# Strassen-Winograd MLP: the last group's combinations moved from GpSimd to VectorE and spread over the products, row and column factor in one instruction

## The chip, the cores and the metric

The kernel runs on one core of a Trainium2 chip. The metric is the device time of one execution in microseconds. Each kernel is timed in several runs; the kernel before has a median of 1384.01 us over 3 runs (1383.27 to 1384.59). A profiled execution gives the trace, with instruction starts counted from the start of its span.

## The reference

A decoder layer on x (1024 tokens x 1024 features, all float32): a mixer (state-space heads and stick-breaking attention heads), cross-attention to 256 memory tokens, a squared-ReLU MLP, each added to the residual h, and one final RMSNorm. The change lies in the MLP's second product and the final norm:

```python
def rmsnorm(x, g):
    y = xf * lax.rsqrt(jnp.mean(xf * xf, axis=-1, keepdims=True) + EPS)
    return (y * g)

def sqrelu_mlp(hn, w1, w2):
    u = hn @ w1                       # 1024 x 4096
    u = jnp.square(jax.nn.relu(u))
    return u @ w2                     # 1024 x 1024

h = h + sqrelu_mlp(rmsnorm(h, norm_ff_g), w_ff1, w_ff2)
return rmsnorm(h, final_g)
```

## The kernel before

The MLP uses the Strassen-Winograd scheme for 2 x 2 blocks: seven block products in place of eight, with sums and differences of blocks before and after them. Each float32 operand is split into a high part (`whi`, a rounded copy made by ScalarE) and a low part (`wlo`, the difference, made by VectorE, line 109), and a product of two operands is three matmuls (lines 207 to 209): high by high, high by low, low by high.

The first stage, a loop over 16 pairs `p` of feature blocks (from line 1165), computes u and stores, for each pair, seven combinations of its blocks in DRAM (`ud`: A11, A12, A22, S1, S2, S3, S4). The four combinations S1, S3, S2, S4 are made on GpSimd (`SE`, line 1163).

The second stage (line 1284) runs over two groups `g` of 8 pairs. In each group come seven products (`prod2`) in the order S3, S1, S2, A11, A22, S4, A12. A product has 8 pairs of operands (one loaded from `ud`, the other a combination of w2's blocks, made in place on VectorE), four row tiles `tb` of 128 rows, and three matmuls for each pair and row tile: 96 matmuls of 128x512. Its four results lie in four PSUM banks; two sets of four banks alternate. When a product is done, `accumulate` adds each bank to its targets: S3's to A7, S1's to A5, S2's to U2, A11's to U2 and C11, A22's is taken off C21, S4's is added to C12 and A12's to C11. C11, C12 and C21 start from the residual h, which three DMAs of 1 MB bring in (line 1226, ahead of both groups).

In the last group (`fin`), after the fourth product, the combinations follow: A7 += U2, C21 += A7 on GpSimd, A7 += A5 and A7 += c22 on VectorE, where c22 is the residual of the fourth quarter, loaded there (line 1322); A7 then holds C22. After the fifth product the final norm of rows 4 to 7 (the lower half: C21 and C22) is worked out, and A5 += U2 and C12 += A5 run on GpSimd. After the seventh product, `last` adds each row tile of C11 and finishes rows 0 to 3. Its matmuls are ordered so that each row tile's last three pairs run together (`NLAST`), so the four row tiles end one after another.

The final norm of a row tile: ScalarE's `squares` sums the squares of each half into the two columns of a small tile `st`; `rows_out` (line 1269) adds them, scales, takes the power -0.5 on GpSimd, and multiplies each half by the row factor `st[:, 3:4]` before the store on SP's queue. The multiplication by the column factor (`gained`, the gain `gfin`) goes ahead of it, on GpSimd or VectorE.

The order of instructions on each engine is worked out when the program is built: a planner takes, among the instructions that are ready in its own model of the time, the one that comes first in the program. `later(by)` moves a stretch in this order: `later(-EARLY)` (3000 places earlier) puts loads and splits of operands ahead, `later(-TB * tb)` does so for the last row tiles. On the chip each engine then works through its list strictly in order. The splits run ahead of the matmuls as far as six buffers of `whi` and `wlo` allow, three pairs of operands.

Of the kernel before, what the change touches and what calls it, by code (L numbers as in the profile page):

```python
# [13 lines left out]
ALU = mybir.AluOpType  # L14
AX = mybir.AxisListType

P = 128
# [22 lines left out]
XQ2 = 1  # L40
XSC = 0
# [49 lines left out]
def hybrid_trunk(ctx: ExitStack, tc: tile.TileContext, xT, x, cols, rows, gain, fing, wzd, wp, out):  # L91
# [1071 lines left out]
    SE = nc.gpsimd  # L1163
    h1 = hp.tile([P, 2, 4, 512], F32, tag="h1", name="w1r2")
    for p in range(NPR):
# [39 lines left out]
        store_u(p, "A22", a22_)  # L1205
        add(s1, a21_, a22_, SE)
# [18 lines left out]
    for c, r, n in ((accs[0][:, 0], 0, 0), (accs[0][:, 1], 0, 1), (accs[1][:, 0], 1, 0)):  # L1225
        nc.sync.dma_start(out=c, in_=hd[rows[r], rows[n]].rearrange("(a p) n -> p a n", p=P))
# [20 lines left out]
    def into(*targets, first=False, sign=ALU.add):  # L1247
        def accumulate(tb, ps):
            for c in targets:
                if first:  # L1250
                    act(c[tb], ps)
                else:
                    tt(c[tb], c[tb], ps, sign)
        return accumulate
# [8 lines left out]
    def gained(t, c, n, eng, gfin):  # L1263

        o = dt_("c", NCB)
        tt(o, c[t % 4], gfin[:, 512 * n:512 * n + 512], ALU.mult, eng)
        return o

    def rows_out(t, obs, st):
        tt(st[:, 2:3], st[:, 0:1], st[:, 1:2], ALU.add)  # L1270
        ts(st[:, 2:3], st[:, 2:3], 1.0 / D, EPS, ALU.mult, ALU.add)
        nc.gpsimd.tensor_tensor(out=st[:, 3:4], in0=st[:, 2:3], in1=nhalf[:, 0:1], op=ALU.pow)
        for n, ob in enumerate(obs):
            ts(ob, ob, st[:, 3:4], None, ALU.mult)
            nc.sync.dma_start(out=out[t * P:(t + 1) * P, 512 * n:512 * n + 512], in_=ob)
# [8 lines left out]
    for g in range(NG):  # L1284
# [25 lines left out]
        if fin:  # L1310
            pl_, tag = slots[2]
            gfin = pl_.tile([P, 2, 4, 512], F32, tag=tag, name="gfin")[:, 0, 0:2].rearrange("p a n -> p (a n)")
            nc.scalar.dma_start(out=gfin, in_=fing.partition_broadcast(P))
        prod2(q, both("S3", lambda a, b, c, d: sub(dt_(("u2", "u3")[next_(nd)], 2), d, b), load),
              into(A7, first=first))
        prod2(q + 1, both("S1", lambda a, b, c, d: sub(b, b, a)), into(A5, first=first))
        prod2(q + 2, both("S2", lambda a, b, c, d: sub(b, d, b)), into(U2, first=first))
        prod2(q + 3, both("A11", lambda a, b, c, d: a), into(U2, C11))
        if fin:
            c22 = [dt_("c", NCB) for _ in range(4)]  # L1320
            for tb in range(4):
                nc.sync.dma_start(out=c22[tb], in_=hd[512 + tb * P:512 + (tb + 1) * P, 512:1024])
                add(A7[tb], A7[tb], U2[tb], nc.gpsimd)
                add(C21[tb], C21[tb], A7[tb], nc.gpsimd)
                tt(A7[tb], A7[tb], A5[tb], ALU.add)
                tt(A7[tb], A7[tb], c22[tb], ALU.add)
        prod2(q + 4, both("A22", lambda a, b, c, d: sub(b, b, c)), into(C21, sign=ALU.subtract))
        if fin:
            for tb in range(4):
                t = 4 + tb  # L1330
                st = squares(t, C21, 0, squares(t, A7, 1))
                rows_out(t, (gained(t, C21, 0, nc.vector, gfin), gained(t, A7, 1, nc.gpsimd, gfin)), st)
                add(A5[tb], A5[tb], U2[tb], nc.gpsimd)
                add(C12[tb], C12[tb], A5[tb], nc.gpsimd)
        prod2(q + 5, both("S4", lambda a, b, c, d: d), into(C12))

        if fin:
            sts = [squares(tb, C12, 1) for tb in range(4)]
            g12 = [gained(tb, C12, 1, nc.gpsimd, gfin) for tb in range(4)]

        def last(tb, ps):
            with later(-TB * tb):
                tt(C11[tb], C11[tb], ps, ALU.add)
                if fin:
                    squares(tb, C11, 0, sts[tb])
                    rows_out(tb, (gained(tb, C11, 0, nc.vector if tb >= GV else nc.gpsimd, gfin), g12[tb]), sts[tb])
# [66 lines left out]
```

## Time and profile before

| | |
|---|---|
| median of 3 runs | 1384.01 us |
| the profiled execution's own time | 1381.92 us |
| its span | 1380.2 us |
| TensorE (PE) busy | 1313.0 us, 95% |
| VectorE (DVE) busy | 972.9 us, 70% |
| ScalarE (ACT) busy | 685.3 us, 50% |
| GpSimd (POOL) busy | 235.6 us, 17% |
| TensorE's granted clock, mean | 0.991 of full speed |

Busy shares are averages over stages with different limits. The stages that the change touches are the end of the first stage (about 1020 to 1080), and the last group of the second stage with the final norm (about 1200 to 1380). PE is TensorE's matmuls and PEld its weight loads; SP only issues DMAs. A matmul of 128x512 shows a duration of about 0.39 us, but they are pipelined and start about 0.23 us apart.

### The profile page before, as it was taken

How to read it: one execution, taken by the hardware profiler on the slowest of the kernel's cores; microseconds unless marked ns; L12 is line 12 of the kernel's file. 1: busy time of each engine (PE TensorE's matmuls, PEld its weight loads, DVE VectorE, ACT ScalarE, POOL GpSimd, SP SyncE). 2: the span in 40 equal slices, each digit the busy share in tenths (PEclk: the TensorE clock that was granted, in tenths of full speed). 3: DMA queues.
4: the chain of work that ended last, by engine and by line, in shares of the span. 5: the costliest groups of instructions: out<-in, count | busy, mean ns of one | idle time of the engine just before them, and what ended most of it. 6: DMA issues, size and time to landing. Idle time of an engine off the chain costs nothing.

```text
span 1380.2 us, 18343 instructions
## 1 busy us (share of the span) xinstructions
PE 1313.0 (95%) x6469; PEld 1065.1 (77%) x6469; DVE 972.9 (70%) x1521; ACT 685.3 (50%) x1304; POOL 235.6 (17%) x238
## 2 busy tenths in 40 slices
PE   9999999899998999999898999999999999999987
PEld 7989977687776778887676888888887888888765
DVE  7748864676789765628789666666659855677896
ACT  7355642565567542626555545554444544444343
POOL 0000002210211010000263323321331000000543
PEclk9999999999999999999998999999999999999999
DMA  6111355842656433111224445444368933633232
GB/s 216 39 62 48 103 152 132 240 117 66 168 162 203 132 108 104 47 31 31 92 77 146 167 153 168 131 144 153 130 208 297 320 113 92 236 92 94 75 124 90
DMA packets 95852, 181.68 MB, mean 132 GB/s; under 512 B 9808, under 2 KB 14992, under 8 KB 95760
## 3 DMA queue, kind: packets, MB, share of 16 engines
q1 hardware_dynamic: 85184, 156.04, 35.3%
q0 software_dynamic: 8624, 18.88, 4.9%
q10 hardware_dynamic: 1952, 5.58, 1.1%
q8 instruction: 51, 0.84, 0.2%
q14 instruction: 41, 0.34, 0.1%
HBM read 128.00 MB, written 52.46 MB: 131 GB/s over the span
## 4 chain that ended last, share of the span: by engine, by line
PE 72%; DVE 12%; issue 6%; ACT 4%; DMA 3%; POOL 2%; POOLq 0%; SPq 0%; DVEq 0%; ACTq 0%
PE P L207 7%; PE P L209 7%; PE P L208 7%; PE pr L207 6%; PE pr L208 6%; PE pr L209 6%; DVE stay L738 3%; DVE wlo L109 3%; PE o L209 2%; PE o L207 2%; PE o L208 2%; DMA wst<-in_wp 2%; PE ops L769 1%; PE wT L755 1%; PE qkps L207 1%
## 5 line engine op out<-in xcount | busy, mean ns | idle before, releaser
L208 PE MATMUL pr<-wlo,whi 128*128 128x512 f32 x448 | 177.7, 397 | 11.4 <-DVE wlo L109 11.3
L207 PE MATMUL pr<-whi 128*128 128x512 f32 x448 | 176.4, 396 | 0.7 <-ACT whi L106 0.7
L209 PE MATMUL pr<-whi,wlo 128*128 128x512 f32 x448 | 177.0, 395 | 0.0
L109 POOL TENSOR_TENSOR c<-c 128x512 f32<-128x512 f32 x64 | 88.9, 1400 | 247.6 <-ACT c L106 223.8
L208 PEld LDWEIGHTS pr<-wlo,whi 128*128 128x128 f32 x448 | 84.3, 188 | 35.2 <-DVE wlo L109 15.9
L109 DVE TENSOR_TENSOR wlo<-w1r,whi 128x512 fp32r<-128x512 f32 x92 | 80.7, 878 | 39.9 <-ACT whi L106 39.7
L106 ACT ACTIVATE whi<-w1r 128x512 fp32r<-128x512 f32 x92 | 58.0, 631 | 94.6 <-PE P L208 62.6
L207 PE MATMUL P<-T,whi 128*128 128x512 f32 x256 | 101.6, 397 | 2.0 <-ACT T L106 2.0
L209 PE MATMUL P<-T,wlo 128*128 128x512 f32 x256 | 101.2, 395 | 0.0
L208 PE MATMUL P<-T,whi 128*128 128x512 f32 x256 | 101.0, 394 | 0.0
L207 PEld LDWEIGHTS pr<-whi 128*128 128x128 f32 x448 | 84.3, 188 | 21.1 <-ACT whi L106 1.1
L209 PEld LDWEIGHTS pr<-whi,wlo 128*128 128x128 f32 x448 | 84.3, 188 | 19.7
L106 ACT ACTIVATE c<-c 128x512 f32<-128x512 f32 x128 | 78.7, 628 | 26.4 <-DVE c L109 25.0
L738 DVE TENSOR_TENSOR_SCAN stay<-stay,dg 128x128 f32<-128x128 f32 (+3 forms) x64 | 84.8, 1346 | 3.9 <-ACT stay L106 3.8
L106 ACT ACTIVATE whi<-wst 128x512 fp32r<-128x512 f32 (+1 forms) x88 | 54.1, 628 | 65.3 <-PE o L209 24.6
L106 ACT ACTIVATE whi<-us 128x512 fp32r<-128x512 f32 x64 | 40.3, 629 | 82.9 <-PE pr L208 74.2
L207 PE MATMUL P<-B,whi 128*128 128x512 f32 x192 | 76.8, 400 | 0.0
L208 PE MATMUL P<-B,whi 128*128 128x512 f32 x192 | 76.4, 398 | 0.0
L209 PE MATMUL P<-B,wlo 128*128 128x512 f32 x192 | 76.3, 397 | 0.0
L109 DVE TENSOR_TENSOR wlo<-wst,whi 128x512 fp32r<-128x512 f32 (+1 forms) x88 | 60.5, 705 | 20.8 <-ACT whi L106 20.5
L109 DVE TENSOR_TENSOR wlo<-pair,whi 128x512 fp32r<-128x512 f32 x96 | 74.4, 775 | 0.0
L109 DVE TENSOR_TENSOR wlo<-us,whi 128x512 fp32r<-128x512 f32 x64 | 47.6, 744 | 36.1 <-ACT whi L106 35.9
(332 smaller groups left out, 3425.6 us busy)
## 6 DMA issues: line engine op xcount, KB each, us to landing
ud<-c SPq DMA_DIRECT2D x112, 256.0 KB, 2.5
wst<-in_wp SPq DMA_DIRECT2D x104, 256.0 KB, 2.8
w1r<-in_wp SPq DMA_DIRECT2D x16, 1024.0 KB, 6.4
us<-ud SPq DMA_DIRECT2D x64, 256.0 KB, 2.6
pair<-in_wp SPq DMA_DIRECT2D x16, 1024.0 KB, 6.5
kk<-kd POOLq DMA_DIRECT2D x32, 256.0 KB, 5.1
p<-ud SPq DMA_DIRECT2D x24, 256.0 KB, 2.6
u<-ud SPq DMA_DIRECT2D x24, 256.0 KB, 2.6
```

Of the source, the lines that this page charges most:

```text
L106: nc.scalar.activation(out=out, in_=in_, func=func, **kw)
L109: (eng or nc.vector).tensor_tensor(out=out, in0=a, in1=b, op=op)
L207: nc.tensor.matmul(out=ps, lhsT=a[0], rhs=b[0], start=start, stop=False)
L208: nc.tensor.matmul(out=ps, lhsT=a[0], rhs=b[1], start=False, stop=False)
L209: nc.tensor.matmul(out=ps, lhsT=a[1], rhs=b[0], start=False, stop=stop)
L738: nc.vector.tensor_tensor_scan(out=stay[:, 0:W][:, ::-1], data0=stay[:, 0:W][:, ::-1], data1=B.dg1[:, S - W:S][:, ::-1], initial=0.0, op0= ...
L755: nc.tensor.transpose(out=t4[:, o:o + P], in_=wb[ii][:, b * P:(b + 1) * P], identity=ident)
L769: nc.tensor.matmul(out=ops[:, oc:oc + 256], lhsT=v, rhs=w[:, sb * 256:sb * 256 + 256], start=(s2_ == 0 and sb == 0 and j == 0), stop=(last ...
```

## The change

The last group's combinations all run on VectorE, each behind the product that gives its summand: after S3, C21 and C22 get A7; after S1, C12 and C22 get A5; after A11, C22, C21 and C12 get U2. C22 is now a tile of its own, loaded with the residual before the last group's first product. `then` calls these additions for each row tile, `AFT` = 24 places later in the order. The first stage's last pair makes its four combinations on VectorE. The loads of C11, C12 and C21 are issued behind the first group's second product. In the final norm, `rows_out` multiplies by row and column factor in one VectorE instruction (`stt`, line 115) in place; for the last row tile alone the column factor goes ahead, VectorE scales one half and ScalarE the other, which is stored by ScalarE's queue. `squares` and `rows_out` of rows 4 to 7 are also `AFT` places later.

```diff
+AFT = 24
-    SE = nc.gpsimd
...
+        SE = nc.gpsimd if p < NPR - 1 else nc.vector
         add(s1, a21_, a22_, SE)
...
-    for c, r, n in ((accs[0][:, 0], 0, 0), (accs[0][:, 1], 0, 1), (accs[1][:, 0], 1, 0)):
-        nc.sync.dma_start(out=c, in_=hd[rows[r], rows[n]].rearrange("(a p) n -> p a n", p=P))
...
-    def into(*targets, first=False, sign=ALU.add):
+    def into(*targets, first=False, sign=ALU.add, then=None):
...
+            if then is not None:
+                with later(AFT):
+                    then(tb)
...
+    def rows_out(t, cs, st):
+
+        factor(t, st)
+        for n, c in enumerate(cs):
+            stt(c[t % 4], c[t % 4], st[:, 3:4], gfin[:, 512 * n:512 * n + 512], ALU.mult, ALU.mult)
+            store_rows(t, n, c[t % 4])
...
+        C22 = [dt_("c", NCB) for _ in range(4)] if fin else None
+
+        def plus(c, a):
+            def go(tb):
+                for c_ in c:
+                    add(c_[tb], c_[tb], a[tb])
+            return go if fin else None
+
+        if fin:
+            for tb in range(4):
+                nc.sync.dma_start(out=C22[tb], in_=hd[512 + tb * P:512 + (tb + 1) * P, 512:1024])
         prod2(q, both("S3", lambda a, b, c, d: sub(dt_(("u2", "u3")[next_(nd)], 2), d, b), load),
-              into(A7, first=first))
-        prod2(q + 1, both("S1", lambda a, b, c, d: sub(b, b, a)), into(A5, first=first))
+              into(A7, first=first, then=plus((C21, C22), A7)))
+        prod2(q + 1, both("S1", lambda a, b, c, d: sub(b, b, a)),
+              into(A5, first=first, then=plus((C12, C22), A5)))
+        if first:
+            for c, r, n in ((accs[0][:, 0], 0, 0), (accs[0][:, 1], 0, 1), (accs[1][:, 0], 1, 0)):
+                nc.sync.dma_start(out=c, in_=hd[rows[r], rows[n]].rearrange("(a p) n -> p a n", p=P))
         prod2(q + 2, both("S2", lambda a, b, c, d: sub(b, d, b)), into(U2, first=first))
-        prod2(q + 3, both("A11", lambda a, b, c, d: a), into(U2, C11))
-        if fin:
-            c22 = [dt_("c", NCB) for _ in range(4)]
-            for tb in range(4):
-                nc.sync.dma_start(out=c22[tb], in_=hd[512 + tb * P:512 + (tb + 1) * P, 512:1024])
-                add(A7[tb], A7[tb], U2[tb], nc.gpsimd)
-                add(C21[tb], C21[tb], A7[tb], nc.gpsimd)
-                tt(A7[tb], A7[tb], A5[tb], ALU.add)
-                tt(A7[tb], A7[tb], c22[tb], ALU.add)
+        prod2(q + 3, both("A11", lambda a, b, c, d: a), into(U2, C11, then=plus((C22, C21, C12), U2)))
...
-            for tb in range(4):
-                t = 4 + tb
-                st = squares(t, C21, 0, squares(t, A7, 1))
-                rows_out(t, (gained(t, C21, 0, nc.vector, gfin), gained(t, A7, 1, nc.gpsimd, gfin)), st)
-                add(A5[tb], A5[tb], U2[tb], nc.gpsimd)
-                add(C12[tb], C12[tb], A5[tb], nc.gpsimd)
+            with later(AFT):
+                for tb in range(4):
+                    st = squares(4 + tb, C21, 0, squares(4 + tb, C22, 1))
+                    rows_out(4 + tb, (C21, C22), st)
...
-                    squares(tb, C11, 0, sts[tb])
-                    rows_out(tb, (gained(tb, C11, 0, nc.vector if tb >= GV else nc.gpsimd, gfin), g12[tb]), sts[tb])
+                    st = squares(tb, C11, 0, sts[tb])
+                    if tb < 3:
+                        rows_out(tb, (C11, C12), st)
+                    else:
+                        g11 = gained(C11[tb], 0)
+                        factor(tb, st)
+                        ts(g11, g11, st[:, 3:4], None, ALU.mult)
+                        act(g12, g12, scale=st[:, 3:4])
+                        store_rows(tb, 0, g11)
+                        nc.scalar.dma_start(out=out[tb * P:(tb + 1) * P, 512:1024], in_=g12)
```

## Rows read from the trace of the kernel before

**Rows 1.** The page's chain that ended last, shares of the span by engine.

```profile
PE 72%; DVE 12%; issue 6%; ACT 4%; DMA 3%; POOL 2%; POOLq 0%; SPq 0%; DVEq 0%; ACTq 0%
```

**Rows 2.** Stretches: us, each engine's busy us (instructions), PEclk, DMA share, GB/s.

```profile
1060.00:1100.00 40.00, 39.33 (x169) 31.41 (x169) 34.59 (x54) 23.16 (x42) 1.54 (x1) 1.00 0.92 313
1222.90:1245.20 22.30, 22.30 (x97) 18.02 (x96) 17.93 (x29) 9.23 (x16) 0.00 (x0) 1.00 0.32 95
1245.20:1267.50 22.30, 22.30 (x97) 18.02 (x96) 17.20 (x28) 9.23 (x16) 0.00 (x0) 1.00 0.32 96
1267.50:1289.80 22.30, 22.30 (x97) 18.02 (x96) 12.66 (x21) 9.22 (x16) 0.00 (x0) 1.00 0.32 95
1289.80:1326.00 36.20, 27.74 (x111) 20.99 (x110) 36.20 (x33) 11.79 (x24) 31.32 (x19) 0.95 0.20 58
```

**Rows 3.** Waits of PE and PEld, 1289 to 1372: us, times, longest.

```profile
PE pr L208 <- DVE wlo L109: 9.2, 6, 3.2
...
PEld pr L208 <- DVE wlo L109: 13.0, 8, 3.6
```

**Rows 4.** Order of time, last group: start us, us, instruction [idle before].

```profile
1267.54 1.88 DVE L109 TENSOR_TENSOR acc<-acc,pr 128x512 f32<-128x512 f32 x3
...
1289.83 1.88 DVE L109 TENSOR_TENSOR acc<-acc,pr 128x512 f32<-128x512 f32 x3
...
1299.35 1.78 DVE L109 TENSOR_TENSOR wlo<-pair,whi 128x512 fp32r<-128x512 f32 x1
...
1300.55 1.75 POOL L109 TENSOR_TENSOR c<-c,acc 128x512 f32<-128x512 f32 x1
...
1301.06 0.68 DVE L109 TENSOR_TENSOR acc<-acc,pr 128x512 f32<-128x512 f32 x1
```

**Rows 5.** Order of time: the last product's end and after it.

```profile
1369.87 0.40 PE L209 MATMUL pr<-whi,wlo 128*128 128x512 f32 x1
...
1367.24 1.98 DVE L113 TENSOR_SCALAR c<-c,fst 128x512 f32<-128x512 f32 x2
...
1370.54 0.68 DVE L109 TENSOR_TENSOR acc<-acc,pr 128x512 f32<-128x512 f32 x1
...
1374.92 0.14 DVE L113 TENSOR_SCALAR fst<-fst 128x1 f32<-128x1 f32 x1
...
1375.15 0.55 POOL L1272 TENSOR_TENSOR fst<-fst,nhalf 128x1 f32<-128x1 f32 x1 [1.13 <-DVE fst L113]
...
1375.73 0.88 DVE L113 TENSOR_SCALAR c<-c,fst 128x512 f32<-128x512 f32 x2 [0.66 <-POOL fst L1272]
```

**Rows 6.** Order of time: between the first and second stage.

```profile
1052.14 2.39 DVE L109 TENSOR_TENSOR u<-pair 128x512 f32<-128x512 f32 x2
1054.45 1.78 DVE L109 TENSOR_TENSOR pair<-pair 128x512 f32<-128x512 f32 x1
1056.16 1.75 DVE L109 TENSOR_TENSOR wlo<-us,whi 128x512 fp32r<-128x512 f32 x1
...
1052.52 4.84 POOL L109 TENSOR_TENSOR c<-c 128x512 f32<-128x512 f32 x3 [22.86 <-ACT c L106]
...
1058.57 0.50 PE L208 MATMUL pr<-wlo,whi 128*128 128x512 f32 x1 [2.13 <-DVE wlo L109]
```

**Rows 7.** Order of time: first load of C11, C12, C21.

```profile
1087.85 0.37 SPq L1226 DMA_DIRECT2D acc<-hd  x1
```

**Rows 8.** Groups by line and form: names, count | busy us, mean ns.

```profile
L116 DVE SCALAR_TENSOR_TENSOR h<-o,ry,h 128x512 f32<-128x512 f32 x16 | 12.0, 747 | 7.6 <-PE o L209 7.4
...
L109 POOL TENSOR_TENSOR c<-acc,gfin 128x512 f32<-128x512 f32 x6 | 8.6, 1446 | 18.6 <-DVE acc L109 18.6
...
L109 POOL TENSOR_TENSOR c<-c,gfin 128x512 f32<-128x512 f32 x4 | 6.4, 1620 | 0.0
...
L106 ACT ACTIVATE u<-acc 128x512 f32<-128x512 f32 x4 | 2.5, 631 | 8.1 <-DVE acc L109 7.2 <-DVE fst L113 0.9
L106 ACT ACTIVATION_READ_ACCUMULATOR u<-acc 128x1 f32 x4 | 0.7, 186 | 0.0
```

More of the change, by code (lines that the diff above doesn't have):

```diff
@@ L1261, in squares, with factor @@
         return st
[L1263 to L1269, printed above, removed]
+    def factor(t, st):
         tt(st[:, 2:3], st[:, 0:1], st[:, 1:2], ALU.add)
@@ L1272, in rows_out, with store_rows, gained @@
         nc.gpsimd.tensor_tensor(out=st[:, 3:4], in0=st[:, 2:3], in1=nhalf[:, 0:1], op=ALU.pow)
-        for n, ob in enumerate(obs):
-            ts(ob, ob, st[:, 3:4], None, ALU.mult)
-            nc.sync.dma_start(out=out[t * P:(t + 1) * P, 512 * n:512 * n + 512], in_=ob)
+    def store_rows(t, n, c):
+        nc.sync.dma_start(out=out[t * P:(t + 1) * P, 512 * n:512 * n + 512], in_=c)
+    def rows_out(t, cs, st):
[3 more added lines that the diff above has]
+            store_rows(t, n, c[t % 4])
+    def gained(c, n):
+        o = dt_("c", NCB)
+        tt(o, c, gfin[:, 512 * n:512 * n + 512], ALU.mult)
+        return o
     NG = NPR // GRP
@@ L1335, in hybrid_trunk @@
         prod2(q + 5, both("S4", lambda a, b, c, d: d), into(C12))
         if fin:
-            sts = [squares(tb, C12, 1) for tb in range(4)]
-            g12 = [gained(tb, C12, 1, nc.gpsimd, gfin) for tb in range(4)]
+            with later(AFT):
+                sts = [squares(tb, C12, 1) for tb in range(4)]
+                g12 = gained(C12[3], 1)
         def last(tb, ps):
```

## The prediction

> **What bounds the kernel now.** I read the chain of waits first: TensorE holds 72% of it, VectorE 12% [rows 1]. So time is lost where VectorE holds TensorE up. The table by stretches finds the place. Three products of the MLP's last group, 1222.9 to 1289.8, keep TensorE busy throughout, beside 29, 28 and 21 VectorE instructions; the stretch 1289.8 to 1326.0, in which the fifth runs, is 36.2 long, and VectorE is busy in all of it with only 33 instructions [rows 2]. From there to the last product's end matmuls waited 9.2 us and weight loads 13.0 us for `wlo`, the low half of an operand's split on VectorE [rows 3]; the two overlap, and neither is the whole loss.
>
> The loss itself: the first accumulations of two undisturbed products start at 1267.54 and 1289.83, so a product takes 22.29 us [rows 4]. Three more from 1289.83 would end at 1356.7; the last matmul starts at 1369.87 and ends at 1370.27 [rows 5]. So 13.6 us are lost in the last three products. Why VectorE is slow there: a split takes 1.78 us with GpSimd at work on an addition (1300.55, 1.75 us), an accumulation that reads PSUM takes 0.68 in the same time, and three such in a row 1.88, thus 0.60 from start to start when nothing is in the way [rows 4]. So it is GpSimd's work, 31.3 us of it there [rows 2], that makes VectorE's instructions on SBUF almost three times as long. After the last matmul another 9.9 us pass.
>
> **The change, part by part.** The sum is made against the profiled execution, 1381.92 us (span 1380.2 and 1.7 around it); the median of the three runs is 2.09 higher, so the forecast for the median is the same gain off 1384.01.
>
> *Combinations.* Sixteen additions leave GpSimd (four each of A7+U2, C21+A7, A5+U2, C12+A5) and eight leave VectorE (A7+A5, A7+c22). Instead VectorE gets 8 after the first product, 8 after the second, 12 after the fourth: 28 x 0.60 = 16.9 us. In which room? The undisturbed products have 29, 28 and 21 instructions [rows 2]; with the new ones the second holds 37, the third 36, the fourth 21. The fifth holds 16 splits, 8 accumulations of the fourth and 12 additions, 36. At 0.60 each that is 22.3, 21.7, 12.7 and 21.7 us of 22.3: full, never over, and additions are deferred by 24 places in the order while splits come 3000 early, so what doesn't fit slides to the fourth or the sixth product. The sixth has 20 and the eight final instructions of rows 4 to 7 (below). The splits run up to three pairs ahead (six buffers, 2.79 us of matmuls a pair), which takes up a few instructions out of turn. So nearly all of the 13.6 us goes. What is late next is VectorE itself: I leave 1.5 us of stalls for three products without slack and take 12.1. Bounds: 13.6, if nothing stalls; and with every addition exposed 16.9 of new stall in its place, -3.3. I take a value near the upper end because in the nearest row, the fully busy 1060 to 1100 before (54 instructions, 34.6 of 40 us), TensorE still runs 39.3 [rows 2].
>
> *Last pair of the first product on VectorE.* Four GpSimd additions there (three in 4.84 us from 1052.52) become four on VectorE, 2.4 us. With GpSimd running, a combination takes 1.78 and a split 1.75, and behind that split TensorE stands 2.13 us [rows 6]. VectorE loses 1.1 us on each of these two and as much on two more of that stretch (1052.14, two in 2.39), 3.3 together, against the 2.4 that it now gets, and those yield to splits. Gain between 0 and 2.1; below nothing it can't go while 2.4 replaces 3.3. I take 1.5, nearer the stall's row, as the additions have no hurry.
>
> *Loads of C11, C12, C21 moved behind the second product.* Three DMAs of 1 MB; the first issued at 1087.85 before [rows 7], in a stretch with the DMA engines 92% busy [rows 2]. They pass loads of operands on SP's queue, which can only come sooner for it. The last group begins three products before 1267.54, at 1200.7, and the first use, the accumulation of the first group's fourth product, lies three before that, at 1133.8: 46 us after the old issue. The 4 loads of c22 likewise only move ahead of a group whose products take 22.3 us each. I take 0 (bounds: 0 and the 0.7 us by which TensorE beside it runs short in 40).
>
> *Final factors.* Before, VectorE had 16 scalings (two in 0.88, 0.40 from start to start) [rows 5] and six multiplications by the gain at 0.60, and GpSimd ten at 1.4 to 1.6 [rows 8]: 10.0 us of VectorE. After: 14 joint instructions, two multiplications, one scaling; ScalarE scales the last half row (0.63, by the square of the same shape [rows 8]). A joint instruction of that size takes 0.747 [rows 8], so about 0.67 from start to start: 14 x 0.67 + 1.2 + 0.4 = 11.0. The eight of rows 4 to 7 (5.4 us) lie beside the last two products, which have room. On the price bears the Trainium skill, "VectorE: DVE Perf Modes", section "The perf-mode tier table (the rule you actually need)": an fp32 scaling from SBUF runs two elements a cycle, an instruction with two tensors one. By that rule joining is no gift where the other half was free on GpSimd, and the trace agrees (0.40 against 0.60 and 0.67); with a joint instruction at the price of a multiplication, 0.60, VectorE's part would be 10.0 and not 11.0, and the sum the same, as the last two products hide either.
>
> *Tail.* T is 1370.27. Before, the last scalings ended at 1376.61, T + 6.3, and the end came 3.6 later [rows 5]. The chain for the last row tile: accumulation 0.68, square 0.63 and its read 0.19 [rows 8], two small ones 0.3, pow 0.55, scaling 0.48: 2.8, with six hand-overs of about 0.1 (from VectorE at 1374.92, 0.14 long, to the pow at 1375.15 it is 0.09 [rows 5]), 3.4. Before it was longer because VectorE stood behind waits: the accumulation of the third tile started at 1370.54, 2.4 us after its matmuls (T - 2.1), behind scalings of which two took 1.98 beside GpSimd, not 0.88 [rows 5]. That 1.1 goes; but the third tile's two joint instructions (1.4) still stand between, and wait for their own pow. I take T + 4.7. The last two stores then go out on two queues, one issue (0.4, as in [rows 7]) less: 3.2. Tail 7.9 for 9.9: gain 2.0. Bounds: 3.3 (the bare chain, 3.4 + 3.2), and -1.6 (no wait goes and six joint instructions cost 0.27 more each).
>
> **Sum.** 12.1 + 1.5 + 0 + 2.0 = 15.6: profiled execution 1366.3, median **1368.4**.
>
> **The rivals.**
> 1. *VectorE becomes the bound.* Three products at 36 to 37 instructions; if each instruction costs its full 0.68 and not 0.60, as where the next has to wait for the one before (accumulation, then an addition to the same tile), a product takes 25.0: 2.7 x 3 = 8.1 of stall, less the 1.5 counted: 1375.0. For it: no undisturbed product held more than 29 [rows 2]. Against: independent instructions lie between.
> 2. *The tail gives nothing.* Rows 0 to 2 now need two joint instructions each after the pow, with 0.27 more apiece; the order of VectorE is fixed ahead, and if it again puts a wait for the pow before an accumulation, 9.9 stays or becomes 11.5: 1370.4 to 1372.0. The tail's rows neither bear this out nor exclude it. The tier rule of the Trainium skill ("VectorE: DVE Perf Modes", "The perf-mode tier table (the rule you actually need)") points to this side.
> 3. *The change doesn't spread what it says.* The 24 places are few; if additions and the finals of rows 4 to 7 gather at the end, the eight joint instructions (5.4) come before the last accumulations: 1373.8. Against: the last two products hold 20 instructions each, 12.1 of 22.3 us.
> 4. *Slower.* The additions are put ahead of the splits that TensorE needs next, and VectorE, in order, exposes them: 16.9, and the eight joint ones 5.4, 22.3 in all against the 17.1 gained (13.6, 1.5, 2.0): 1389.2. It decides from about 77% exposed. Against it is the order before, in which accumulations stand between pairs of splits at 1289.83 and 1301.06 [rows 4] and not ahead of them.
>
> **Numbers.** The forecast has 0.59; rival 2 0.15; rival 1 0.15; rival 3 0.07; rival 4 0.04. The range goes down to 1364, about the sum of all upper bounds (13.6 + 2.1 + 0.7 + 3.3 = 19.7 gives 1364.3), and up to 1376, which takes in rivals 1 and 3. A measurement tells about 0.2%, 2.8 us: faster 0.92 (the forecast and rivals 1 to 3 make 0.96, of which 0.04 goes to same, for their far ends), same 0.04, slower 0.04.
>
> **What would show it.** GpSimd without 128x512 additions after 1290, splits at 0.7 us throughout, TensorE without waits for `wlo` in the last three products and products of 22.3 us: right. Splits still late though each is short: rival 1. Over 9 us between last matmul and end: rival 2. Joint instructions of rows 4 to 7 after the last matmul: rival 3. The forecast is wrong if the fifth product stays above 26 us.

## The result and the profile after

The kernel after takes 1370.18 us (median of 4 runs, 1368.33 to 1371.06) and the kernel before, run beside it, 1383.64 (4 runs, 1381.3 to 1384.59): ratio 0.9903, 95% interval 0.9891 to 0.9915. The forecast was 1368.4, within 1364 to 1376. The profiled execution after takes 1368.33 us with a span of 1366.6, so 13.6 us of span have gone.

To see where, I cut the span of every kernel below at the same events. *Transition* runs from the start of the first stage's last `u<-P,p` on VectorE (the sum of a product in PSUM and `p1`; 1036.72 before, 1036.85 after) to the start of the last group's first accumulation into `c` (1222.92, 1222.17); it takes in the end of the first stage, the whole first group and the first product of the last. *Group* runs from there to the end of the last matmul, over the other six products; *tail* from there to the end of the span. The time ahead of the first event moves by 2 us and more between profiles of one and the same code, so effects of about 1 us are read from these stretches and not from the total.

| kernel | transition | group | tail | profiled execution | median of runs (range), ratio to before with its 95% interval |
|---|---|---|---|---|---|
| before | 186.20 | 147.35 | 9.93 | 1381.92 | |
| after | 185.32 | 135.15 | 9.28 | 1368.33 | 1370.18 (1368.33 to 1371.06), 0.9903 [0.9891, 0.9915] |
| after_again | 185.54 | 135.13 | 9.28 | 1369.22 | 1370.81 (1369.22 to 1371.28), 0.9904 [0.9888, 0.9921] |
| e1_spread_pool | 186.41 | 147.02 | 9.27 | 1381.63 | 1381.46 (1380.27 to 1383.43), 0.9988 [0.9976, 0.9999] |
| e2_gather_dve | 185.59 | 135.15 | 9.32 | 1370.38 | 1369.96 (1369.77 to 1370.38), 0.9898 [0.9874, 0.9921] |
| e3_se_pool | 186.84 | 135.14 | 9.34 | 1371.68 | 1370.71 (1368.09 to 1371.68), 0.9901 [0.9878, 0.9923] |
| e4_loads_front | 186.04 | 135.15 | 9.26 | 1368.35 | 1370.9 (1368.35 to 1373.0), 0.9904 [0.988, 0.9928] |
| e5_old_tail | 185.82 | 135.15 | 9.89 | 1370.53 | 1370.87 (1370.53 to 1371.51), 0.9916 [0.9899, 0.9932] |
| e6_tail_act | 185.76 | 135.14 | 8.64 | 1366.6 | 1368.2 (1366.6 to 1368.89), 0.9893 [0.9879, 0.9908] |
| e7_adds_first | 184.81 | 135.14 | 9.31 | 1370.09 | 1370.37 (1368.55 to 1372.53), 0.9911 [0.9896, 0.9926] |
| e9_double | 186.17 | 135.17 | 9.32 | 1369.9 | 1370.32 (1368.88 to 1373.18), 0.9913 [0.9898, 0.9928] |
| e8_tail_mix | 185.66 | 135.13 | 8.02 | 1367.19 | 1367.49 (1366.35 to 1369.12), 0.9884 [0.9864, 0.9904] |
| e10_us4 | 182.91 | 135.13 | 9.31 | 1367.2 | 1365.87 (1365.37 to 1367.2), 0.9872 [0.9856, 0.9888] |
| e11_all | 184.24 | 135.13 | 7.99 | 1368.01 | 1366.75 (1363.92 to 1368.01), 0.9874 [0.9855, 0.9893] |

So from before to after 12.20 us are gained in the group, 0.88 in the transition and 0.65 in the tail. The group and the tail repeat within 0.1 wherever their code is the same. The transition does not: nine profiles with its code unchanged (after, after_again, e1, e2, e5 to e9) range from 184.81 to 186.41, and 186.20 before lies among them. The 0.88 is therefore not told apart from nothing. The labels of the rows below "after" are those of the experiments.

The page of the kernel after: its engines (busy us, share, instructions) and its chain that ended last.

```profile
PE 1309.2 (96%) x6469; PEld 1064.7 (78%) x6469; DVE 957.7 (70%) x1540; ACT 686.8 (50%) x1305; POOL 188.7 (14%) x208
...
PE 77%; DVE 9%; issue 6%; ACT 3%; DMA 2%; POOL 2%; SPq 0%; POOLq 0%; ACTq 0%; DVEq 0%
```

TensorE's share of the chain rises from 72% to 77% and VectorE's falls from 12% to 9% [rows 1]. VectorE's busy time falls too, from 972.9 to 957.7 us, although it does more instructions (1540 for 1521): its instructions have become shorter on average.

The table by stretches of the kernel after, in steps of a product (22.30), the answer to [rows 2]; columns as there. A stretch begins with the accumulation of a product that has just ended, so the second product of the group runs in the first stretch and the fifth in the fourth.

```profile
1222.20:1244.50 22.30, 22.30 (x98) 18.02 (x97) 22.02 (x38) 9.24 (x16) 0.00 (x0) 1.00 0.31 95
1244.50:1266.80 22.30, 22.30 (x98) 18.01 (x97) 21.40 (x37) 9.25 (x16) 0.00 (x0) 1.00 0.33 96
1266.80:1289.10 22.30, 22.30 (x98) 18.03 (x97) 12.66 (x22) 9.24 (x16) 0.00 (x0) 1.00 0.31 95
1289.10:1311.40 22.30, 22.30 (x98) 18.02 (x97) 21.79 (x37) 11.97 (x25) 0.00 (x0) 1.00 0.33 94
1311.40:1333.70 22.30, 22.30 (x97) 18.01 (x96) 18.66 (x38) 11.56 (x24) 2.69 (x4) 1.00 0.57 190
1333.70:1357.30 23.60, 23.60 (x101) 18.51 (x99) 15.19 (x28) 11.55 (x26) 1.10 (x2) 1.00 0.10 34
```

TensorE is busy in all of it, at the full granted clock; the stretch that showed 0.95 and 27.74 of 36.2 us before is gone. Beside the second to the fifth product VectorE holds 38, 37, 22 and 37 instructions, 22.02, 21.40, 12.66 and 21.79 us. The waits of TensorE's matmuls between 1200 and 1360 have no row left, where before 9.2 us stood for `wlo` [rows 3]. The same columns for the whole group of the kernel before:

```profile
1222.92:1370.27 147.35, 138.12 (x581) 108.75 (x579) 121.00 (x173) 61.66 (x120) 46.55 (x32) 0.99 0.29 90
```

After, TensorE's busy time there is 135.15, the whole stretch. So of the 12.20 gained, 9.23 are time in which TensorE stood still, and 2.97 are matmuls that took longer: between 1320 and 1324 its granted clock was 0.57 before, mostly the lower of its two levels (1.2 GHz), after 4 us in which it was busy for 1.19. How the 2.97 divide between the clock and the restarts behind each wait I have not worked out.

The order of time on VectorE in the fifth product of the kernel after (start, us, instruction), to be held against [rows 4].

```profile
1289.08 1.88 DVE L110 TENSOR_TENSOR acc<-acc,pr 128x512 f32<-128x512 f32 x3
...
1298.64 0.69 DVE L110 TENSOR_TENSOR acc<-acc 128x512 f32<-128x512 f32 x1
1299.24 0.69 DVE L110 TENSOR_TENSOR wlo<-p,whi 128x512 fp32r<-128x512 f32 x1
1299.84 0.69 DVE L110 TENSOR_TENSOR wlo<-pair,whi 128x512 fp32r<-128x512 f32 x1
1300.44 0.69 DVE L110 TENSOR_TENSOR acc<-acc,acc 128x512 f32<-128x512 f32 x1
```

An addition, two splits and an addition start 0.60 apart, 0.69 each; a split was 1.78 at this place before.

The transition of the kernel after, in order of time, the answer to [rows 6].

```profile
1053.48 0.69 DVE L110 TENSOR_TENSOR pair<-pair 128x512 f32<-128x512 f32 x1
...
1053.78 0.63 ACT L107 ACTIVATE whi<-us 128x512 fp32r<-128x512 f32 x1 [1.20 <-DMA us<-ud]
...
1054.45 0.69 DVE L110 TENSOR_TENSOR wlo<-us,whi 128x512 fp32r<-128x512 f32 x1 [0.28 <-ACT whi L107]
...
1057.45 0.69 DVE L110 TENSOR_TENSOR c<-c 128x512 f32<-128x512 f32 x1
...
1060.13 1.20 PE L208 MATMUL pr<-whi 128*128 128x512 f32 x4 [0.99 <-ACT whi L107]
```

And the waits of its TensorE from 1040 to 1300 (us in total, times, longest).

```profile
PE pr L208 <- ACT whi L107: 2.0, 2, 1.0
```

The combination of w2's blocks takes 0.69, not 1.78, the split 0.69, not 1.75, and the stall of 2.13 us behind it is gone. But new waits stand in its place: TensorE waits twice for `whi`, the other half of the split, and ScalarE, which makes it, had waited 1.20 us for the DMA that brings `us` from DRAM. In the whole transition TensorE is idle for 1.97 us, and for 2.80 before.

The three loads of the residual go out on SP at 1082.71, 1085.44 and 1091.52; the first went out at 1087.85 before [rows 7].

The tail of the kernel after, in order of time, from the last matmuls; T, the end of the last matmul, is 1357.32. Of [rows 5] this is the answer.

```profile
1356.68 0.75 DVE L117 SCALAR_TENSOR_TENSOR acc<-acc,fst,gfin 128x512 f32<-128x512 f32 x1 [0.66 <-POOL fst L1269]
1356.92 0.40 PE L210 MATMUL pr<-whi,wlo 128*128 128x512 f32 x1
...
1357.42 0.75 DVE L117 SCALAR_TENSOR_TENSOR acc<-acc,fst,gfin 128x512 f32<-128x512 f32 x1
1358.08 0.69 DVE L110 TENSOR_TENSOR acc<-acc,pr 128x512 f32<-128x512 f32 x1
...
1358.91 0.99 POOL L1269 TENSOR_TENSOR fst<-fst,nhalf 128x1 f32<-128x1 f32 x1 [2.26 <-DVE fst L114]
1359.40 0.19 ACT L107 ACTIVATION_READ_ACCUMULATOR u<-acc 128x1 f32 x1
1359.93 0.75 DVE L117 SCALAR_TENSOR_TENSOR acc<-acc,fst,gfin 128x512 f32<-128x512 f32 x1 [0.44 <-POOL fst L1269]
1360.60 0.15 DVE L110 TENSOR_TENSOR fst<-fst 128x1 f32<-128x1 f32 x1
1360.67 0.75 DVE L117 SCALAR_TENSOR_TENSOR acc<-acc,fst,gfin 128x512 f32<-128x512 f32 x1
1361.33 0.15 DVE L114 TENSOR_SCALAR fst<-fst 128x1 f32<-128x1 f32 x1
1361.56 0.55 POOL L1269 TENSOR_TENSOR fst<-fst,nhalf 128x1 f32<-128x1 f32 x1 [1.66 <-DVE fst L114]
1362.15 0.72 ACT L107 ACTIVATE c<-c,fst 128x512 f32<-128x512 f32 x1 [2.56 <-POOL fst L1269]
```

The last accumulation starts at 1358.08, T + 0.76, behind the two joint instructions of the second tile, the first of which waits 0.66 for its power on GpSimd (the pow). ScalarE has the sum of squares of the last tile at 1359.59, but the small addition that needs it starts at 1360.60, behind the third tile's first joint instruction, and its partner at 1361.33, behind the second one: 1.0 and about 0.6 us of queue on VectorE. The last scaling, ScalarE's, takes 0.72 and ends at 1362.87, T + 5.55, and the span 3.73 later.

### The profile page after: what moved, and what is told of

Read it like the earlier page. It is cut to its first block, busy times and chain, and to the rows that moved or that the text cites. A ratio compares the mean times of both kernels' runs of the same rounds, so it can differ in the third digit from the quotient of the medians.

```text
span 1366.6 us, 18308 instructions
## 1 busy us (share of the span) xinstructions
PE 1309.2 (96%) x6469; PEld 1064.7 (78%) x6469; DVE 957.7 (70%) x1540; ACT 686.8 (50%) x1305; POOL 188.7 (14%) x208
## 4 chain that ended last, share of the span: by engine, by line
PE 77%; DVE 9%; issue 6%; ACT 3%; DMA 2%; POOL 2%; SPq 0%; POOLq 0%; ACTq 0%; DVEq 0%
PE pr L208 8%; PE pr L209 8%; PE pr L210 7%; PE P L208 7%; PE P L210 7%; PE P L209 7%; DVE stay L739 4%; PE o L210 2%; PE o L208 2%; PE o L209 2%; PE ops L770 1%; PE qkps L208 1%; PE qkps L210 1%; PE qkps L209 1%; DMA wst<-in_wp 1%
## 5 line engine op out<-in xcount | busy, mean ns | idle before, releaser
L110 POOL TENSOR_TENSOR c<-c 128x512 f32<-128x512 f32 x60 | 84.7, 1422 | 201.2 <-ACT c L107 198.8
L110 DVE TENSOR_TENSOR wlo<-w1r,whi 128x512 fp32r<-128x512 f32 x92 | 77.2, 840 | 43.5 <-ACT whi L107 43.5
L110 DVE TENSOR_TENSOR wlo<-us,whi 128x512 fp32r<-128x512 f32 x64 | 44.6, 696 | 36.6 <-ACT whi L107 36.0
L756 PE MATMUL wT<-ident,stay 128*128 128x128 f32 x288 | 51.3, 282 | 16.2 <-DVE stay L739 15.0
```

The lines of the kernel that those rows point to most:

```text
L110: (eng or nc.vector).tensor_tensor(out=out, in0=a, in1=b, op=op)
L756: nc.tensor.transpose(out=t4[:, o:o + P], in_=wb[ii][:, b * P:(b + 1) * P], identity=ident)
```

## The experiments

Each kernel differs from the kernel after by the lines shown. The questions: is it GpSimd or the gathering that cost the 12 us (e1, e2); what are the two other moves worth (e3, e4); where did the tail's gain go (e5, e6, e8); has VectorE room (e7, e9); and what does the new wait cost (e10, e11).

**e1, spread as after, but the additions on GpSimd.**

```
-                    add(c_[tb], c_[tb], a[tb])
+                    add(c_[tb], c_[tb], a[tb], nc.gpsimd)
```

> The kernel after the change, with its 28 additions behind the first, second and fourth product of the last group given to GpSimd instead of VectorE; their places in the order stay. Theory S (the two engines get in each other's way on SBUF): each addition takes 1.6 to 1.7 us on GpSimd and slows the VectorE instructions beside it by 1.1 us each, about 8 us of VectorE in each of the second and third product and 12 in the fifth; stalls of 8 to 13 us come back and the time is 1378 to 1383, with splits of 1.7 to 1.8 us in the trace. Rival G (the combinations were only too dense in one place): spread out they fit on either engine, 1370 to 1372.

The group takes 147.02, nearly the whole gain is lost: 0.9988 of before. The stretch of the second product in this kernel's table:

```profile
1222.20:1244.50 22.30, 20.12 (x86) 15.65 (x85) 21.96 (x25) 8.13 (x15) 13.58 (x8) 1.00 0.27 75
```

VectorE in it, in order of time:

```profile
1226.53 1.78 DVE L110 TENSOR_TENSOR wlo<-pair,whi 128x512 fp32r<-128x512 f32 x1
1228.23 0.67 DVE L110 TENSOR_TENSOR c<-c,pr 128x512 f32<-128x512 f32 x1
...
1229.93 1.78 DVE L110 TENSOR_TENSOR wlo<-u,whi 128x512 fp32r<-128x512 f32 x1
1231.64 1.78 DVE L110 TENSOR_TENSOR wlo<-pair,whi 128x512 fp32r<-128x512 f32 x1
```

GpSimd at the same time:

```profile
1226.01 1.75 POOL L110 TENSOR_TENSOR c<-c 128x512 f32<-128x512 f32 x1
1227.71 1.75 POOL L110 TENSOR_TENSOR acc<-acc,c 128x512 f32<-128x512 f32 x1
```

And TensorE's waits from 1200 to 1390 (us, times, longest):

```profile
PE pr L209 <- DVE wlo L110: 7.9, 6, 2.0
```

In 22.30 us VectorE gets through 25 instructions, and is as full (21.96) as with the 38 of the kernel after. Splits take 1.78 and start 1.70 apart, in step with GpSimd's additions; the accumulation, which reads PSUM, stays at 0.67. The Trainium skill, "SBUF — State Buffer", section "SBUF: two separate sides", says that a VectorE instruction with two SBUF inputs and a GpSimd instruction that reads SBUF lock each other out for a whole instruction. The trace agrees in kind, by the distance of 1.70 from start to start against 0.60 alone; in size 1.70 is less than the 0.60 and the 1.30 that a GpSimd addition took alone (1290.59 before) add up to. So spreading by itself is worth nothing; the engine is what counts.

**e2, gathered as before, but all on VectorE.**

```
-              into(A7, first=first, then=plus((C21, C22), A7)))
+              into(A7, first=first))
...
-        prod2(q + 3, both("A11", lambda a, b, c, d: a), into(U2, C11, then=plus((C22, C21, C12), U2)))
+        prod2(q + 3, both("A11", lambda a, b, c, d: a), into(U2, C11))
+        if fin:
+            for tb in range(4):
+                add(A7[tb], A7[tb], U2[tb])
+                add(C21[tb], C21[tb], A7[tb])
+                add(A7[tb], A7[tb], A5[tb])
+                add(C22[tb], C22[tb], A7[tb])
...
                     rows_out(4 + tb, (C21, C22), st)
+                    add(A5[tb], A5[tb], U2[tb])
+                    add(C12[tb], C12[tb], A5[tb])
```

> The kernel after, with the combinations gathered again as before (16 additions behind the fourth product, 8 behind the fifth), all of them on VectorE. Theory S: no GpSimd beside it, so splits stay at 0.7 us; the fifth product holds 40 VectorE instructions, 24.1 us at 0.60, against 22.3, so 1 to 4 us of stalls and 1371 to 1374. Rival G: gathering was the fault, most of the 13.6 us comes back, 1380 to 1383.

The group takes 135.15, as after, and no matmul waits in it; no stall of the 1 to 4 us expected. The spreading that gives the change its name is not what gains: with 24 gathered additions VectorE keeps up just as well, once GpSimd is quiet.

**e3, the first stage's last combinations back on GpSimd.**

```
-        SE = nc.gpsimd if p < NPR - 1 else nc.vector
+        SE = nc.gpsimd
```

> The kernel after, with the first stage's last pair's four combinations on GpSimd again. Theory S: the stall of 2.1 us between the stages comes back and another of about 1 us there stays or goes; the last group starts 0.7 to 1.5 us later, 1371 to 1371.7. Rival (the loads' new place gave the gain there): no later start, 1370.2.

The old stall returns, as TensorE's waits from 1040 to 1300 of this kernel show:

```profile
PE pr L209 <- DVE wlo L110: 2.1, 1, 2.1
```

The transition takes 186.84, against 185.32 and 185.54 in the two profiles of the kernel after: 1.3 to 1.5 more. But this is not time that TensorE waits. The transition of this kernel and of the kernel after, and a stretch behind the stall, in the columns of the table by stretches:

```profile
1038.68:1225.52 186.84, 184.72 (x788) 148.48 (x787) 134.36 (x207) 84.68 (x149) 6.44 (x4) 0.99 0.61 199
1036.85:1222.17 185.32, 183.35 (x788) 147.44 (x787) 132.53 (x210) 84.80 (x149) 0.00 (x0) 1.00 0.60 201
1062.00:1064.00 2.00, 2.00 (x6) 1.32 (x4) 1.93 (x4) 1.70 (x4) 0.00 (x0) 0.50 0.87 304
```

TensorE is idle for 2.12 us here and for 1.97 and 2.15 in the two profiles of the kernel after: the stall for `wlo` takes the place of the two waits for `whi`, at the same size. What is longer is its busy time, 184.72 against 183.35. Behind the stall (busy for 0.40 of the 2 us from 1058) the granted clock falls to 0.50, the lower level; the kernel before has the same stall of 2.13 and no such fall there. So the move of the four combinations exchanged one wait for another, and one profile of each can't tell what it is worth beyond that. The runs (0.9901) don't show it either.

**e4, the three loads put back ahead of both groups.**

```
     A5 = [a5[:, tb, :] for tb in range(4)]
+    for c, r, n in ((accs[0][:, 0], 0, 0), (accs[0][:, 1], 0, 1), (accs[1][:, 0], 1, 0)):
+        nc.sync.dma_start(out=c, in_=hd[rows[r], rows[n]].rearrange("(a p) n -> p a n", p=P))
...
-        if first:
-            for c, r, n in ((accs[0][:, 0], 0, 0), (accs[0][:, 1], 0, 1), (accs[1][:, 0], 1, 0)):
-                nc.sync.dma_start(out=c, in_=hd[rows[r], rows[n]].rearrange("(a p) n -> p a n", p=P))
```

> The kernel after, with the three loads of C11, C12 and C21 in their old place ahead of both groups. My theory: they are off the path, the last group starts within 0.2 us of the kernel after, 1370.2. Rival: they compete with operand loads between the stages, where the DMA engines are 90% busy, and the start is 0.5 to 0.9 us later.

No effect that shows: group 135.15, transition 186.04, within the scatter. The trace says why. SP issues the three loads at 1082.90, 1085.46 and 1091.54, against 1082.71, 1085.44 and 1091.52 after. The place in the program moved and the place in time did not, so it is not their place in the program that moved the first of them from 1087.85 in the kernel before.

**e5, the final norm of rows 0 to 3 as before.**

```
-                g12 = gained(C12[3], 1)
+                g12 = [dt_("c", NCB) for _ in range(4)]
+                for tb in range(4):
+                    tt(g12[tb], C12[tb], gfin[:, 512:1024], ALU.mult, nc.gpsimd)
...
+                    g11 = dt_("c", NCB)
+                    tt(g11, C11[tb], gfin[:, 0:512], ALU.mult, nc.vector if tb >= GV else nc.gpsimd)
+                    factor(tb, st)
+                    for n, o in enumerate((g11, g12[tb])):
+                        ts(o, o, st[:, 3:4], None, ALU.mult)
+                        store_rows(tb, n, o)
```

> The kernel after, with the final norm of rows 0 to 3 as before (column factor ahead, on GpSimd for the second half of all four tiles and the first half of two; one scaling each behind the pow). Theory: the joint form and GpSimd's work weigh about the same there; the time from the last matmul to the end goes from 9.3 back to 9.9 us, and the GpSimd multiplications beside the last product slow splits there to 1.7 us without a wait of TensorE over 0.5 us: 1370.5 to 1371.5. Rival: the joint form is what the tail gained and more was hidden, 1372 or above.

The tail is 9.89, the 9.93 of before again. So the 0.65 lies in these lines and nothing else gave to the tail. The stretch of the last product shows one thing more:

```profile
1333.70:1357.30 23.60, 23.60 (x102) 18.85 (x101) 17.71 (x23) 11.67 (x26) 9.12 (x7) 1.00 0.05 15
```

GpSimd is busy for 9.12 us of it with the multiplications that came back, and the splits beside these take up to 1.79 again, but no matmul waits: VectorE has room there (17.71 of 23.60). GpSimd's work beside VectorE costs time only where VectorE is filled by it, as far as these runs show. The four multiplications that rows 4 to 7 had on GpSimd before are in no run by themselves.

**e6, one joint instruction a tile, ScalarE scales the other half.** The column factor of C12 goes ahead for all four tiles.

```
-                g12 = gained(C12[3], 1)
+                for tb in range(4):
+                    tt(C12[tb], C12[tb], gfin[:, 512:1024], ALU.mult)
...
-                        rows_out(tb, (C11, C12), st)
+                        factor(tb, st)
+                        stt(C11[tb], C11[tb], st[:, 3:4], gfin[:, 0:512], ALU.mult, ALU.mult)
+                        g11 = C11[tb]
...
+                    act(C12[tb], C12[tb], scale=st[:, 3:4])
+                    store_rows(tb, 0, g11)
+                    nc.scalar.dma_start(out=out[tb * P:(tb + 1) * P, 512:1024], in_=C12[tb])
```

> The kernel after, with the column factor of the second half of rows 0 to 3 multiplied in beside the last product on VectorE, and its row factor applied by ScalarE behind the pow; VectorE keeps one joint instruction per row tile. Theory Q (the tail is VectorE's queue: in the kernel after the third tile's pow waits behind the second's joint instructions): three joint instructions (2.0 us) leave it, of which 1 to 1.6 us show: 7.7 to 8.3 us from the last matmul to the end, 1368.6 to 1369.2. Rival W (the tail is the chain of one row tile, its pow and its store): 9.2 us and no change.

The tail falls to 8.64, between the 7.7 to 8.3 expected and the rival's 9.2. With one instruction in place of two behind each pow, the queue on VectorE is shorter; by the trace the last tile's small addition starts at 1358.02, but its partner only at 1359.43, behind the third tile's joint instruction (1358.77, 0.75).

**e8, as little as possible behind a pow on VectorE.** As e6, but from the second tile on the column factor of C11 goes ahead too, the second tile is scaled by ScalarE alone, the third and fourth by half each, and all stores go out on SP.

```
-                    if tb < 3:
-                        rows_out(tb, (C11, C12), st)
+                    if tb == 0:
+                        factor(tb, st)
+                        stt(C11[tb], C11[tb], st[:, 3:4], gfin[:, 0:512], ALU.mult, ALU.mult)
+                        g11 = C11[tb]
                     else:
...
+                    if tb == 1:
+                        act(g11, g11, scale=st[:, 3:4])
+                    if tb >= 2:
                         ts(g11, g11, st[:, 3:4], None, ALU.mult)
...
+                    act(C12[tb], C12[tb], scale=st[:, 3:4])
+                    store_rows(tb, 0, g11)
+                    store_rows(tb, 1, C12[tb])
```

> The kernel after, with the final norm of rows 0 to 3 arranged so that VectorE stands behind a pow less: ScalarE applies the row factor to the second half of every row tile and to both halves of the second, the column factor is multiplied in ahead. Theory Q (VectorE's queue holds up the pow of the last tile): the third tile's accumulation no longer waits for the second's pow; 8.0 to 8.5 us from the last matmul to the end (8.6 with one joint instruction per tile left on VectorE). Rival: ScalarE's queue takes its place, since its scalings stand before the last squares: 9 us.

The tail is 8.02, 1.26 less than after, and its order of time shows the queue gone:

```profile
1357.08 0.40 PE L210 MATMUL pr<-whi,wlo 128*128 128x512 f32 x1
...
1357.98 0.49 DVE L114 TENSOR_SCALAR c<-c,fst 128x512 f32<-128x512 f32 x1 [0.66 <-POOL fst L1269]
...
1358.39 0.68 DVE L110 TENSOR_TENSOR acc<-acc,pr 128x512 f32<-128x512 f32 x1
...
1359.96 0.16 DVE L110 TENSOR_TENSOR fst<-fst 128x1 f32<-128x1 f32 x1 [0.17 <-ACT u L107]
...
1360.97 0.72 ACT L107 ACTIVATE acc<-acc,fst 128x512 f32<-128x512 f32 x1 [1.04 <-POOL fst L1269]
```

The small addition now waits for ScalarE, not for VectorE's queue, and the last scaling ends at 1361.69, T + 4.21 (T is 1357.48). What is left before the last accumulation is a scaling that waits 0.66 for the third tile's pow. So behind the last pows the column factor ahead, where VectorE idles, and a scaling of 0.49 behind, with more of the scaling on ScalarE, are together cheaper than the joint form; how the 1.26 divide among these moves no run shows.

**e7, additions ahead of the splits.**

```
-                with later(AFT):
+                with later(-2 * EARLY):
```

> The kernel after, with the 28 additions put 6000 places ahead in the order, before the splits, instead of 24 behind. Theory S: VectorE has room for them wherever they stand, since splits run up to three pairs ahead; at most 1 us of waits, 1370 to 1371. Rival P (the order is what saves it, rival 4 of the prediction in small): the additions delay the splits that come next, 4 us or more of waits for wlo, 1374 or above.

Group 135.14, no matmul waits. The order did change: two or three additions now stand directly behind an accumulation and ahead of the next splits, where in the kernel after splits come between them. So the order of additions and splits is worth nothing here. Rival 4 is met in this form only, since the additions come in twos and threes and never all at once.

**e9, every addition made twice** (56 in place of 28; the output then counts those summands twice).

```
-                for c_ in c:
+                for c_ in c + c:
```

> The kernel after, with each of the 28 additions made twice (the summands count double in the output): 56 on VectorE. It shows how near VectorE is to being the bound. Theory: the second, third and fifth product then hold 45, 44 and 48 instructions, 27, 26.5 and 29 us against 22.3; what is deferred slides to the fourth and later products, which take some 10 us, and 4 to 8 us of 16.9 become waits: 1374 to 1378. Rival (there is room to slide all of it): below 1372. Rival (no room at all): 1385 and above.

The table by stretches of this kernel, third to sixth product:

```profile
1244.50:1266.80 22.30, 22.30 (x98) 18.00 (x97) 22.14 (x37) 9.21 (x17) 0.00 (x0) 1.00 0.31 98
1266.80:1289.10 22.30, 22.30 (x98) 18.02 (x97) 21.33 (x36) 9.24 (x17) 0.00 (x0) 1.00 0.33 94
1289.10:1311.40 22.30, 22.30 (x98) 18.04 (x97) 21.43 (x36) 10.00 (x19) 0.00 (x0) 1.00 0.34 95
1311.40:1333.70 22.30, 22.30 (x98) 18.00 (x97) 21.67 (x42) 13.35 (x31) 1.75 (x3) 1.00 0.33 101
```

I had expected 4 to 8 us of waits and there are none: group 135.17. VectorE is full through five stretches on end (21.78 of 22.30 in the one before these), the surplus slides into those that had room (beside the fourth product from 12.66 to 21.33, and in the last stretch from 15.19 to 19.59 of 23.60), and no matmul waits. A VectorE at 96 to 99% held nobody up here; how much more would be too much no run shows.

**The kernel after once more**, for the scatter.

> The kernel after, unchanged, beside the three that follow: 1369.5 to 1370.7 us, 135.1 us from the first product's first accumulation of the last group to the last matmul, 9.3 us from there to the end.

1370.81, stages 185.54, 135.13, 9.28: the group and the tail repeat to 0.02, the transition to 0.2 in this one repetition; the wider scatter of the table counts for it.

**e10, four buffers for `us` in place of two.** Of the operands that a group's first product loads, every second goes into another pair of buffers.

```
-                    us = dt_(("us", "p1", "us", "u4")[j % 4] if load is None else "us", 2)
+                    us = temp("us") if load is not None and j % 2 else dt_(("us", "p1", "us", "u4")[j % 4] if load is None else "us", 2)
```

> The kernel after, with four buffers instead of two for the operand loaded from DRAM in each group's first product (every second one goes into the two tiles that the first stage used for its difference S3). Theory D (between the stages TensorE now waits for this operand's load, as two buffers are refilled in turn): the 2 us of waits for whi there fall below 1 and the last group starts 0.7 to 1.5 us earlier than in the kernel after, 1369 to 1369.5. Rival: the waits are VectorE's and ScalarE's own work at this place, no change.

The transition takes 182.91, 2.4 and 2.6 less than the two profiles of the kernel after and 1.9 less than the shortest of the nine, more than the 0.7 to 1.5 expected; TensorE's waits from 1040 to 1300 have no row left. The table by stretches of the kernel after shows the loss:

```profile
1045.00:1065.00 20.00, 19.00 (x82) 14.91 (x81) 18.96 (x31) 9.13 (x16) 0.00 (x0) 1.00 0.94 332
1065.00:1085.00 20.00, 19.02 (x83) 15.12 (x82) 18.72 (x31) 12.11 (x22) 0.00 (x0) 1.00 0.92 306
```

The same stretches of this kernel:

```profile
1045.00:1065.00 20.00, 20.00 (x88) 15.97 (x87) 19.75 (x33) 10.85 (x19) 0.00 (x0) 1.00 0.91 309
1065.00:1085.00 20.00, 20.00 (x88) 16.17 (x87) 19.70 (x33) 11.17 (x20) 0.00 (x0) 1.00 0.95 327
```

TensorE gets back the 2.0 us that it lost in these 40. The DMA engines are 91 to 95% busy in both: what was short was not their rate but a free buffer to start the load into. At 1365.87, where 1369 to 1369.5 was expected, this is the fastest kernel here, by 4.9 us against the kernel after (1370.81) run on the same chip; the stages account for 2.6 of it, the two profiled executions differ by 2.0, and the rest the traces don't show.

**e11, four buffers and the mixed tail together.**

> The kernel after with both of the edits before (the tail with less of VectorE behind a pow, four buffers for the operand): the two gains add, 1367.5 to 1368.6. If they do not add, one of the two causes is not what it is taken for.

The edits are those of e10 and e8. 1366.75, 0.9874, below the 1367.5 to 1368.6 expected, but not faster than the four buffers alone (0.9872). Against the kernel after beside them, e8 gains 3.3 us, e10 4.9 and both together 4.1: the gains don't add. By stretches the tail's does, 7.99 as alone. The transition is 184.24 and not 182.91; of these 1.33, one wait of TensorE accounts for 1.1, by its waits from 1040 to 1300:

```profile
PE pr L208 <- DVE c L110: 1.1, 1, 1.1
```

The first stage and the transition are the same code in both. Whether such a wait comes and goes with the DMAs' timing, or the longer list of the last product changed the order of loads, one profile of each can't tell; that stays open.

## Why the prediction was right, and where not

**Combinations: 12.1 forecast, 12.20 measured, by two errors that cancel.** The loss of 13.6 was too large: I counted three products from 1289.83, an accumulation of the first row tile. By the kernel after, the last matmul ends 68.24 us behind that instruction (1289.08 to 1357.32), which is three products of 22.29 and 1.37 of the product before. So 12.2 were there to be had. Against it stood 1.5 of new stalls; there were none. That the two errors nearly cancel is luck. The counts of instructions (37, 36, 21, 36 forecast; 38, 37, 22, 37 found, in windows that cut at other places) and their 21 to 22 us were right (the sums with 0.60 come out with 0.603), but the reading that so full a product makes TensorE wait was wrong: doubled additions cost nothing either (e9).

**The cause was as forecast, its name in the change not.** GpSimd beside VectorE made the splits long: the spread additions on GpSimd lose nearly everything (e1), gathered ones on VectorE lose nothing (e2).

**Transition: 1.5 forecast, 0.88 found, which the scatter of 1.6 doesn't tell from nothing.** The stall of 2.13 went as forecast, but the term took its going for gain. What is late next was not named there: `whi` from an operand whose load waits for one of two buffers, 2.0 us, as much as the stall that comes back in e3. Taking that away (e10) yields more than the term itself.

**Loads: 0 forecast, 0 measured,** for a simpler reason than mine: they go out at the same time from either place (e4).

**Tail: 2.0 forecast, 0.65 measured; this is the term that was mis-sized.** I put the last scaling at T + 4.7 and it ended at T + 5.55. The bare chain was about right (3.2 for my 3.4), but I added 1.3 for what stands between, and the trace shows 1.6 inside the chain and 0.76 ahead of the last accumulation, where VectorE waits for the second tile's pow; that wait is the mechanism of rival 2. I had seen that the third tile's two joint instructions "still stand between, and wait for their own pow", but not that they also stand between the two small instructions of the last tile, nor that the third tile's pow takes 0.99 and not 0.55 beside a VectorE multiplication, nor that ScalarE's scaling takes 0.72 and not 0.63. And no saving by the second store queue shows: 3.73 us from the last scaling to the end, where I took 3.2; with both last stores on SP (e8) it is 3.81, and 3.6 before. By my own mark, over 9 us from last matmul to end, rival 2 came true at 9.28, though its price (9.9 to 11.5) did not.

The sum: the profiled execution came 2.0 above the forecast of 1366.3, of which 1.35 is the tail and 0.62 the transition.

**The other rivals.** Rival 1 fell with 37 and 38 instructions a product and no wait, and e9 had none with 36 to 42. Rival 3 fell: the joint instructions of rows 4 to 7 lie beside the last two products, and gathered additions cost nothing (e2). Rival 4 fell with the result, and e7 had no wait with the additions ahead of the splits.

## What to carry to other kernels

Before spreading or reordering work that stalls another engine, ask on which engine it runs: an elementwise addition on GpSimd cost VectorE about 1.1 us for each of its instructions with two SBUF inputs beside it here, more than the 0.6 it would have cost to do the addition on VectorE; GpSimd's work cost time only where VectorE was full by it (e1), not where it had room (e5). A full in-order engine is not yet the bound: with splits up to three pairs ahead of the matmuls, the surplus additions could slide (e9). A stall that is gone is not yet a gain: ask what stood right behind it (e3, e10). At the end of a kernel, where nothing is left to hide behind, count what stands in the queue between the links of the last chain, and do ahead of the last factor whatever doesn't need it.

## What the hardware showed that I had not expected

- GpSimd's power of a 128x1 tile took 0.99 us beside a VectorE multiplication with two SBUF inputs (1358.91) and 0.55 with VectorE idle (1361.56): even a tiny GpSimd instruction is held up. The same pair stands in the kernel before (0.99 at 1373.03, 0.55 at 1375.15).
- The slowing is the same with the additions gathered (before) or spread (e1): 1.70 from start to start for a split beside GpSimd, 0.60 alone, and no effect on instructions that read PSUM (0.67).
- Joining two factors in one instruction (0.75, 0.67 from start to start) gained 0.65 us of tail together with taking GpSimd's halves away (e5); at the very end a multiplication ahead and a scaling of 0.49 behind was better by 1.26 us of tail (9.28 to 8.02), together with ScalarE's share.
